# Attention units of a fused transformer layer issued as a fixed software pipeline

## The chip, the cores and the metric

The program runs on one core of one Trainium2 chip. Its time is the device time of one execution in microseconds (us). It is measured in whole executions; one more execution is recorded by the hardware profiler, and all rows below are of that one. TensorE (PE in the profile) does the matmuls and the transposes, VectorE (DVE) and GpSimd (POOL) elementwise work, ScalarE (ACT) activations and copies, and SyncE (SP) issues the DMAs. Matmuls write to PSUM, eight banks of 512 fp32 columns on 128 partitions.

## The reference

One layer of a hybrid backbone on 640 tokens: 512 latent tokens (group 0) and 128 prompt tokens (group 1). An adaLN map gives shift, scale and gate of each group; the normalised input goes through one input projection to four mixers; their outputs are projected, gated, summed and projected again; a squared-ReLU MLP follows.

```python
sh1, sc1, g1, sh2, sc2, g2 = jnp.split(mod, 6, axis=-1)          # adaLN
h = _rmsnorm(x, P['norm_mix_pre']) * (1 + sc1) + sh1
u = _split_cols(h @ P['w_in'])
o_a, st_a = _hgrn_mixer(u, P, lb_f, lb_b, ctx)                    # gated recurrence, 4 heads
o_b, st_b = _swa_mixer(u, P, pos, ctx)                            # window attention, 8 heads of 64
o_c, st_c = _mla_mixer(u, P, pos, ctx)                            # latent attention, 8 heads of 64 + 32
o_d, st_d = _gqa_mixer(u, P, pos, ctx)                            # grouped attention, 8 heads of 64
y = _merge((o_a, o_b, o_c, o_d), u['gates'], P)                   # sum of sigmoid(gate) * (o @ w_branch), @ w_out
x = x + g1 * _rmsnorm(y, P['norm_mix_post'])
...
y = jnp.square(jax.nn.relu(h @ P['w_mlp_in'])) @ P['w_mlp_out']
x = x + g2 * _rmsnorm(y, P['norm_mlp_post'])
```

Each attention is softmax(q k) v. Prompt tokens read prompt tokens only (128 keys). Latent tokens read 128 cached keys and the 512 latent keys (640 keys); in the window attention the cached ones and those up to 128 tokens away (384 or 512 keys), with a sink logit for each head.

## The kernel before

Activations are stored transposed (features on partitions) as pairs of a high and a low part, and each dense product is three matmuls: high times high, high times low, low times high. `t_steps` (line 357) makes a 128 x 640 block of a projection in two halves of 320 tokens; `tok_block` (line 375) makes a 128-token block in token order. Each weight tile of 512 KB is loaded by SP's queue (`wload`), its high part copied on GpSimd (line 139) and its low part made on VectorE (line 142).

PSUM is in pools: four banks for scores as two tiles of two banks (`sc_tile`, `sc_bank`), two banks for transposes and value products (`tp_tile`, `pv_tile`, one tag), two for projections (`mm_tile`, `mp_tile`, one tag).

The order of the instructions on each engine comes from a planner (it takes what its own costs say is ready, by priority in program order), except inside `in_order(...)`, which chains the named engines' instructions in the order in which the program writes them. Before the change this holds for the start and, for TensorE alone, for the first mixer (HGRN), where `beside(share)` takes so much dense work from a generator at each place. Stages by span time:

- 104 to 300: HGRN, two pairs of heads, seven levels each, with projections and `gate_steps(0)` beside them. A level is a block of matmuls, VectorE's product, two products on GpSimd (line 598), and VectorE again.
- 300 to 326: keys and first queries of the window attention, `merge(0)`. 326 to 478: its units, with the second pair's queries (`queries(1)`) and the gates (`gates(1)`) to be put between them by the planner.
- 478 to 526: keys and first queries of the grouped attention and `merge(1)`. 526 to 684: its units, second queries and `gates(3)`.
- 684 to 797: projections of the latent attention, `merge(3)`, `gates(2)`. 797 to 943: its four head pairs. Each has a prelude, written in front of its five units (lines 1142 to 1174): queries, rotary queries (five transposes), values of two pairs in every other one, keys. The projection banks are closed for this stage; one holds the adaLN accumulators, one is the prelude's `pj_tile`.
- To 1000: `gate_rows` and `merge(2)`; then the output projection, and from 1037 the MLP.

A `unit` (line 800) is one block of 128 queries for two heads: scores; per head a maximum, exponential with sum, reciprocal, and a weighing of P on GpSimd (`weigh`, line 809); transposes of P, four to a bank (line 856), copied out by ScalarE and VectorE in turn (lines 858, 860); value products into a bank of the same tag; `o_evac`. With 640 keys each head has its own two-bank score tile, filled in two pieces of 320. Each stage has 20 units, four of them on prompt tokens (one key tile). The score matmuls of the grouped kinds are two per piece and head (`qk_mm`), those of the latent one three (line 1182).

`q_split` (line 772) writes the high and the low part of a query block from PSUM. `side_steps(n)` runs `n` of the pending adaLN steps: each loads a weight tile of 512 KB and does four matmuls (line 211); in the latent attention three after every unit.

Of the kernel before, what the change touches and what calls it, by code (L numbers as in the profile page):

```python
# [20 lines left out]
T = TS + TP  # L21
# [43 lines left out]
def trunk(ctx, tc, I, O):  # L65
# [26 lines left out]
    pss = ctx.enter_context(tc.tile_pool(name="pss", bufs=2, space=PSUM))  # L92
# [3 lines left out]
    psm = [None, None]  # L96

    def open_mm():
        psm[1] = ExitStack()
        psm[0] = psm[1].enter_context(tc.tile_pool(name="psm", bufs=2, space=PSUM))  # L100

# [6 lines left out]
    def sc_tile():  # L108
        return pss.tile([128, 2, 512], F32, tag="sc", name="sc")
# [247 lines left out]
    def t_steps(w, m0, X, evac, halves=((0, HALF), (HALF, HALF)), bank=mm_tile):  # L357

        nk = len(w)
        for t0, tn in halves:  # L360
            ps = bank()
            for k in range(nk):
                wh, wl = w[k][0][:, m0:m0 + 128], w[k][1][:, m0:m0 + 128]
                a, b = X[k][0][:, t0:t0 + tn], X[k][1][:, t0:t0 + tn]
                PE.matmul(out=ps[:, 0:tn], lhsT=wh, rhs=a, start=(k == 0), stop=False)  # L365
                PE.matmul(out=ps[:, 0:tn], lhsT=wh, rhs=b, start=False, stop=False)  # L366
                PE.matmul(out=ps[:, 0:tn], lhsT=wl, rhs=a, start=False, stop=(k == nk - 1))  # L367
            evac(ps[:, 0:tn], t0, tn)
            yield 1.0
# [126 lines left out]
    V.tensor_scalar(out=nsink, in0=sink_b, scalar1=-1.0, scalar2=None, op0=ALU.mult)  # L496

# [190 lines left out]
    def gate_steps(n, sig):  # L688

        for kk in range(8):  # L690
# [5 lines left out]
            if kk % 4 == 3:  # L696
# [8 lines left out]
    with tc.tile_pool(name="hx", bufs=1) as hx:  # L705
# [25 lines left out]
        fill, due = dense(), 0.0  # L731

        def beside(share):

            nonlocal due
            due += share
            while due > 0:
                due -= next(fill, 100.0)

        with in_order(PE):  # L740
            for hp in range(2):
                lev = hgrn_levels(*qfk[hp], hx)
                while True:
                    try:
                        beside(next(lev))
# [3 lines left out]
                for share in hgrn_out(hp, *qfk[hp], A, QP, hx):  # L749
                    beside(share)  # L750
            for _ in fill:
                pass
# [47 lines left out]
    def unit(n, c, heads, qt, nk, score, pv_mm, sink=False, bands=None):  # L800
# [11 lines left out]
        if W > 512:  # L812

            for i in range(2):
                sv = sc_tile()[:, :, 0:W // 2]
                for a in range(2):
                    score(sv[:, a], i, a * (W // 2), W // 2)
                V.tensor_reduce(out=negm[:, i:i + 1], in_=sv, axis=AX.XY, op=ALU.max, negate=True)
                S.activation(out=Pt[:, i, 0:W].rearrange("p (a n) -> p a n", a=2), in_=sv, func=AF.Exp,
                             bias=negm[:, i:i + 1], accum_out=den[:, i:i + 1])  # L820
                V.reciprocal(out=rden[:, i:i + 1], in_=den[:, i:i + 1])  # L821
                weigh(i)
        else:
            sv = sc_tile()[:, :, 0:W]
# [26 lines left out]
        for j, kt in enumerate(range(0, nk, 2)):  # L851
            kn = min(2, nk - kt)
            tp = tp_tile().rearrange("p (k i) t -> p k i t", i=2)
            for i in range(2):
                for kk in range(kn):
                    PE.transpose(out=tp[:, kk, i], in_=Pt[:, i, 128 * (kt + kk):128 * (kt + kk) + 128], identity=ident)  # L856
            if j % 2 == 0:
                S.activation(out=PT[:, kt:kt + kn], in_=tp[:, 0:kn], func=AF.Copy)
            else:
                V.tensor_copy(out=PT[:, kt:kt + kn], in_=tp[:, 0:kn])  # L860
        o = pv_tile()
        for kt in range(nk):
            for a in range(2):
                pv_mm(o[64 * a:64 * a + 64, 0:128], a, kt, PT[:, kt, a], kt == 0, kt == nk - 1)
        o_evac(n, c, 128 * qt, o[:, 0:128])

    def gqa_like(n, qn, kn, ck, cv, ok, ov_, norm):
# [38 lines left out]
        def queries(j2):  # L906
            QQ = big(F32R, 2, 2, T, name="Q")
            Q = [QQ[:, a] for a in range(2)]
# [3 lines left out]
            for tt in range(NT):  # L912
                x = prepare(tt, ps, 4, norm and norm[0], None)
                if tt + 1 < NT:
                    ps = tok_block(wq, 256, hT, tt + 1, bank())

# [3 lines left out]
                q_split(tp[:, 0:2], [x[:, :, 128 * tt:128 * tt + 128] for x in Q], 0.125)  # L920
            return Q
        return queries, K, Vt
# [67 lines left out]
    def run_gqa(n, queries, Q0, K, Vt, tiles, sink, bands):  # L990
        for j2 in range(2):
            Q = queries(j2) if j2 else Q0
            for qt, i in [(qt, i) for qt in range(5) for i in range(2)]:
                ks, j = tiles(qt), 2 * j2 + i

                def score(out, a, k0, kn):
                    Qa = Q[a][:, i, 128 * qt:128 * qt + 128]
                    done = 0
                    while done < kn:
                        first = ks[(k0 + done) // 128] * 128 + (k0 + done) % 128  # L1000
                        step = 128 - (k0 + done) % 128
                        while done + step < kn and ks[(k0 + done + step) // 128] * 128 == first + step:
                            step += 128
                        step = min(step, kn - done)
                        qk_mm(out[:, done:done + step], Qa, K_part(K, first, step), a)
                        done += step

                def pv_mm(out, a, kt, PTa, start, stop):
                    PE.matmul(out=out, lhsT=Vt[:, ks[kt], 64 * a:64 * a + 64], rhs=PTa, start=start, stop=stop)  # L1009
# [333 lines left out]
```

## Time and profile before

| | |
|---|---|
| median of three executions | 1501.23 us (1500.88 to 1502.49) |
| profiled execution | 1502.2 us, span 1500.4 us, mean granted TensorE clock 0.991 |
| busy share of the span | PE 95%, DVE 53%, ACT 32%, POOL 29% |
| DMA | 121.17 MB, mean 81 GB/s |

The span runs from the first recorded instruction to the last. A busy share is that of the whole span, so it says nothing of a single stage; for that, the stretches below give each engine's busy time between two times of the span. In the chain of waits each step is what released the one after it. In a timeline, the bracket behind an instruction is the idle time of its engine just before it and what ended that.

### The profile page before, as it was taken

The numbers are of one execution on the slowest core, as the hardware profiler recorded it, in microseconds if no ns is written. First come the engines' busy times: TensorE is split into PE (matmuls) and PEld (weight loads), VectorE is DVE, ScalarE is ACT, GpSimd is POOL, SyncE is SP. The second block draws the span as 40 slices with busy tenths as digits, with TensorE's granted clock in tenths as the row PEclk, the third lists the DMA queues.
The fourth block names the chain that finished last, engine by engine and source line by source line (L and its number), as shares of the span: only waits on it lengthen the run. The fifth ranks groups of instructions, "written<-read, shape, count | busy, mean of one in ns | idle before, by whom it ended". The sixth has DMA issues, their size and how long they took to land.

```text
span 1500.4 us, 26709 instructions
## 1 busy us (share of the span) xinstructions
PE 1430.5 (95%) x10969; PEld 1302.2 (87%) x10969; DVE 796.1 (53%) x1447; ACT 481.4 (32%) x1161; POOL 432.2 (29%) x456
## 2 busy tenths in 40 slices
PE   6999999899999999999998998998999999999996
PEld 5898998899898998999996677988898998898995
DVE  4347657476643788433725566746243444444446
ACT  4334333333443235442124565225220110110112
POOL 2015325243321545222213334124111111112114
PEclk9999999999999999999999999999999999999998
DMA  9421212121112131112224601221343223222221
GB/s 328 128 85 58 70 49 64 50 68 50 45 43 59 34 84 37 33 42 74 80 68 143 224 15 43 99 85 56 112 129 101 80 71 98 71 70 71 75 66 70
DMA packets 138225, 121.17 MB, mean 81 GB/s; under 512 B 22296, under 2 KB 119412, under 8 KB 138104
## 3 DMA queue, kind: packets, MB, share of 16 engines
q1 hardware_dynamic: 138104, 119.47, 26.4%
q8 instruction: 86, 1.41, 0.4%
q14 instruction: 35, 0.29, 0.1%
HBM read 115.96 MB, written 3.49 MB: 80 GB/s over the span
## 4 chain that ended last, share of the span: by engine, by line
PE 70%; issue 13%; DVE 8%; POOL 5%; ACT 2%; DMA 1%; POOLq 0%; DVEq 0%; SPq 0%; ACTq 0%
PE mm L365 12%; PE mm L366 11%; PE mm L367 11%; PE mm L381 4%; PE mm L382 4%; PE mm L383 4%; PE tp L856 3%; POOL wh L139 3%; PE pv L1009 3%; PE sc L383 3%; PE sc L381 2%; PE sc L382 2%; PE sc L949 2%; PE sc L950 2%; DVE wl L142 1%
## 5 line engine op out<-in xcount | busy, mean ns | idle before, releaser
L139 POOL TENSOR_SCALAR wh<-wr 128x1024 fp32r<-128x1024 f32 (+3 forms) x136 | 156.7, 1154 | 536.4 <-PE mm L366 290.4
L142 DVE TENSOR_TENSOR wl<-wr,wh 128x1024 fp32r<-128x1024 f32 (+3 forms) x160 | 198.9, 1247 | 160.0 <-POOL wh L139 120.8
L365 PE MATMUL mm<-hTh,wh 128*128 128x320 f32 x704 | 220.5, 313 | 2.0 <-DVE qA L520 0.9
L367 PE MATMUL mm<-hTh,wl 128*128 128x320 f32 x704 | 219.2, 311 | 0.0
L366 PE MATMUL mm<-hTl,wh 128*128 128x320 f32 x704 | 218.2, 310 | 0.0
L366 PE MATMUL mm<-h2Tl,wh 128*128 128x320 f32 x512 | 159.4, 311 | 1.1 <-DVE h2Tl L142 1.1
L365 PE MATMUL mm<-h2Th,wh 128*128 128x320 f32 x512 | 159.5, 312 | 0.0
L367 PE MATMUL mm<-h2Th,wl 128*128 128x320 f32 x512 | 159.2, 311 | 0.0
L809 POOL TENSOR_SCALAR P<-P,rden 128x640 f32<-128x640 f32 (+3 forms) x120 | 84.5, 713 | 184.0 <-DVE rden L821 80.7
L365 PEld LDWEIGHTS mm<-hTh,wh 128*128 128x128 f32 x704 | 132.2, 188 | 3.9 <-DVE qA L520 1.0
L367 PEld LDWEIGHTS mm<-hTh,wl 128*128 128x128 f32 x704 | 132.2, 188 | 0.9 <-issue 0.7
L366 PEld LDWEIGHTS mm<-hTl,wh 128*128 128x128 f32 x704 | 132.2, 188 | 0.5 <-issue 0.3
L382 PE MATMUL mm<-wl,hidh 128*128 128x512 f32 x320 | 124.8, 390 | 0.6 <-DVE wl L142 0.6
L381 PE MATMUL mm<-wh,hidh 128*128 128x512 f32 x320 | 125.3, 392 | 0.0
L383 PE MATMUL mm<-wh,hidl 128*128 128x512 f32 x320 | 124.6, 389 | 0.0
L1292 ACT ACTIVATE relu<-mm 128x320 f32<-128x320 f32 x64 | 28.0, 438 | 281.1 <-PE mm L367 281.1
L366 PEld LDWEIGHTS mm<-h2Tl,wh 128*128 128x128 f32 x512 | 97.1, 190 | 1.7 <-DVE h2Tl L142 1.5
L365 PEld LDWEIGHTS mm<-h2Th,wh 128*128 128x128 f32 x512 | 96.9, 189 | 0.7 <-issue 0.4
L367 PEld LDWEIGHTS mm<-h2Th,wl 128*128 128x128 f32 x512 | 97.0, 189 | 0.0
L1293 DVE TENSOR_TENSOR relu<-relu 128x320 f32<-128x320 f32 x64 | 40.4, 632 | 100.8 <-ACT relu L1292 100.8
L1305 DVE TENSOR_TENSOR y<-mm,y 128x512 f32<-128x512 f32 x70 | 48.2, 689 | 81.9 <-PE mm L383 81.9
L381 PE MATMUL sc<-wh,hTh 128*128 128x256 f32 (+2 forms) x224 | 72.0, 322 | 5.5 <-DVE tx L935 2.4
(355 smaller groups left out, 3238.4 us busy)
## 6 DMA issues: line engine op xcount, KB each, us to landing
wr<-in_w_in SPq DMA_DIRECT2D x56, 512.0 KB, 3.7
wada<-in_w_ada SPq DMA_DIRECT2D x48, 512.0 KB, 4.5
wr<-in_w_mlp_in SPq DMA_DIRECT2D x32, 512.0 KB, 4.0
wr<-in_w_mlp_out SPq DMA_DIRECT2D x32, 512.0 KB, 3.6
wr<-in_w_in SPq DMA_DIRECT2D x64, 64.0 KB, 2.1
wr<-in_w_branch SPq DMA_DIRECT2D x8, 512.0 KB, 4.1
wr<-in_w_branch SPq DMA_DIRECT2D x16, 256.0 KB, 4.1
wr<-in_w_out SPq DMA_DIRECT2D x8, 512.0 KB, 3.6
```

The lines of the kernel that those rows point to most:

```text
L139: G.tensor_scalar(out=out, in0=src, scalar1=1.0, scalar2=1.0, op0=ALU.mult, op1=ALU.mult)
L142: V.tensor_tensor(out=out, in0=src, in1=f(hi), op=ALU.subtract)
L365: PE.matmul(out=ps[:, 0:tn], lhsT=wh, rhs=a, start=(k == 0), stop=False)
L366: PE.matmul(out=ps[:, 0:tn], lhsT=wh, rhs=b, start=False, stop=False)
L367: PE.matmul(out=ps[:, 0:tn], lhsT=wl, rhs=a, start=False, stop=(k == nk - 1))
L381: PE.matmul(out=ps[:, 0:n], lhsT=a, rhs=w[k][0], start=(start and k == 0), stop=False)
L382: PE.matmul(out=ps[:, 0:n], lhsT=a, rhs=w[k][1], start=False, stop=False)
L383: PE.matmul(out=ps[:, 0:n], lhsT=b, rhs=w[k][0], start=False, stop=(stop and k == nk - 1))
L809: G.tensor_scalar(out=Pt[:, i, 0:W], in0=Pt[:, i, 0:W], scalar1=rden[:, i:i + 1], scalar2=1.0, op0=ALU.mult, op1=ALU.mult)
L856: PE.transpose(out=tp[:, kk, i], in_=Pt[:, i, 128 * (kt + kk):128 * (kt + kk) + 128], identity=ident)
L1009: PE.matmul(out=out, lhsT=Vt[:, ks[kt], 64 * a:64 * a + 64], rhs=PTa, start=start, stop=stop)
L1305: V.tensor_tensor(out=ys, in0=ps, in1=ys, op=ALU.add)
```

## The change

Every attention unit is split into three functions: its scores with the softmax, `turn(part)` for the transposes (part 0 the first two banks, part 1 the third) and `products`. `run_units` issues them in rounds, with TensorE's order fixed: scores of a new unit, transposes of the unit before it, value products of the one before that, and after each part of the round a place for dense work. The dense work now comes in quarters of a half block: `t_steps` yields after every second weight block. In the window and the grouped attention `Fill.give(0.34)` at each place takes the second pair's queries and the gates in turn; units of prompt tokens (qt 4) stand third and seventh among the ten of a pair; the gates' sigmoids come after the last unit. In the latent attention the whole prelude of the first pair is made ahead of the units, in `sc_bank` and `mm_tile` in turn; those of the next pairs are the dense work (0.13 a place), two adaLN steps follow each value product, and the prompt unit stands third of five. All of PSUM but the transpose banks is laid out anew there: three banks in a row for the scores of both heads (cut at the banks into pieces of 512, 128, 384 and 256), one for adaLN, two for `pj`. The HGRN stage uses `Fill` too, with the same shares as before.

```diff
     def t_steps(w, m0, X, evac, halves=((0, HALF), (HALF, HALF)), bank=mm_tile):
...
                 PE.matmul(out=ps[:, 0:tn], lhsT=wl, rhs=a, start=False, stop=(k == nk - 1))
+                if k % 2 and k < nk - 1:
+                    yield tn / 1280
             evac(ps[:, 0:tn], t0, tn)
-            yield 1.0
+            yield (2 - nk % 2) * tn / 2560
...
+    class Fill:
...
+        def give(self, share):
+            self.due += share
+            while self.due > 0:
+                self.due -= next(self.steps, 1e9)
...
+        def softmax(i, sv, to, axis):
+            V.tensor_reduce(out=negm[:, i:i + 1], in_=sv, axis=axis, op=ALU.max, negate=True)
+            S.activation(out=to, in_=sv, func=AF.Exp, bias=negm[:, i:i + 1], accum_out=den[:, i:i + 1])
+            V.reciprocal(out=rden[:, i:i + 1], in_=den[:, i:i + 1])
+            weigh(i)
...
+        def wide_in():
+            k = 0
+            while k < 2 * W:
+                i, k0 = k // W, k % W
+                kn = min(W - k0, 512 - k % 512)
+                score(banks[:, k:k + kn], i, k0, kn)
+                k += kn
+            for i in range(2):
+                softmax(i, banks[:, W * i:W * i + W], Pt[:, i, 0:W], AX.X)
...
+        def turn(part):
+            for j, kt in list(enumerate(range(0, nk, 2)))[2 * part:2 * part + 2]:
...
+    def run_units(units, beside, after=lambda: None):
+        cur = old = None
+        units = iter(units)
+        with in_order(PE):
+            while True:
+                new = next(units, None)
+                if new is None and cur is None and old is None:
+                    break
+                if new:
+                    new[0]()
+                if cur:
+                    cur[1](0)
+                beside()
+                if cur:
+                    cur[1](1)
+                beside()
+                if old:
+                    old[2]()
+                    after()
+                beside()
+                old, cur = cur, new
...
+        def query_steps(j2, Q):
...
             for tt in range(NT):
                 x = prepare(tt, ps, 4, norm and norm[0], None)
                 if tt + 1 < NT:
                     ps = tok_block(wq, 256, hT, tt + 1, bank())
+                yield 0.8
...
                 q_split(tp[:, 0:2], [x[:, :, 128 * tt:128 * tt + 128] for x in Q], 0.125)
+                yield 0.1
...
+    def run_gqa(n, query_steps, Q0, K, Vt, tiles, sink, bands):
+        Q1, sig = [], [big(F32, 4, T, name="sig") for _ in range(2)]
+        second = query_steps(1, Q1)
+        def dense():
+            gate = gate_steps(n, sig, True)
+            for i, share in enumerate(second):
+                yield share
+                if i % 2 == 0:
+                    yield next(gate)
+            yield from gate
...
+                for qt, i in ((0, 0), (0, 1), (4, 0), (1, 0), (1, 1), (2, 0), (4, 1), (2, 1), (3, 0), (3, 1)):
...
+        fill = Fill(dense())
+        run_units(units(), lambda: fill.give(0.34))
+        fill.rest()
+        for g in sig:
+            S.activation(out=g, in_=g, func=AF.Sigmoid)
...
+        def heads(jj, got, bank):
...
+        banks = [sc_bank, mm_tile]
+        for _ in heads(0, got[0], lambda: banks.reverse() or banks[0]()):
+            pass
+        psm[1].close()
+        scores = psx.tile([128, 3, 512], F32, name="scores").rearrange("p a n -> p (a n)")
+        preludes = [None] + [heads(jj, got[jj], lambda: psx.tile([128, 512], F32, tag="pj", name="pj", bufs=2))
+                             for jj in range(1, 4)]
...
+                fill.rest()
+                fill.steps, fill.due = (preludes[jj + 1] if jj < 3 else iter(())), 0.0
+                for qt in (0, 1, 4, 2, 3):
+                    yield one(jj, qt, *got[jj])
...
-                side_steps(3)
+        run_units(units(), lambda: fill.give(0.13), lambda: side_steps(2))
```

## Rows read from the trace of the kernel before

**Rows 1.** Page: span; busy time and instructions by engine.
```profile
span 1500.4 us, 26709 instructions
...
PE 1430.5 (95%) x10969; PEld 1302.2 (87%) x10969; DVE 796.1 (53%) x1447; ACT 481.4 (32%) x1161; POOL 432.2 (29%) x456
```

**Rows 2.** Stretches: start:end, length, busy us of PE, PEld, DVE, ACT, POOL, granted clock, DMA.
```profile
104.00:300.00 196.00, 182.91 (x2420) 176.54 (x2419) 122.80 (x159) 74.68 (x154) 80.22 (x46) 1.00 0.22 61
326.00:478.00 152.00, 150.86 (x1153) 137.50 (x1152) 85.70 (x206) 61.52 (x174) 43.13 (x59) 1.00 0.21 53
478.00:526.00 48.00, 43.59 (x331) 42.09 (x331) 30.86 (x82) 14.39 (x34) 21.59 (x27) 0.96 0.17 41
526.00:684.00 158.00, 154.44 (x1285) 145.66 (x1283) 94.58 (x200) 67.42 (x172) 54.93 (x65) 1.00 0.19 49
...
797.00:943.00 146.00, 130.29 (x1122) 100.62 (x1121) 89.77 (x198) 83.29 (x227) 58.30 (x87) 0.98 0.32 105
```

**Rows 3.** Chain that ended last, latent attention: start, duration, work.
```profile
853.47 0.57 PE ada_ps L211 x8
...
886.73 1.96 PE mm L1203 x8
...
892.83 1.02 PE pv L1185 x16
...
925.75 1.02 PE pv L1185 x16
```

**Rows 4.** Timeline of one latent unit: start, duration, engine, line, instructions.
```profile
928.34 0.39 PE L949 MATMUL sc<-mK,mQ 128*128 128x320 f32 x1
...
929.15 0.31 PE L1182 MATMUL sc<-ckv,mQ 128*128 128x320 f32 x1
...
929.30 0.82 PE L856 MATMUL tp<-ident,P 128*128 128x128 f32 x6
...
929.50 0.82 DVE L818 TENSOR_REDUCE negm<-sc 128x1 f32<-128x640 f32 x1 [0.59 <-PE sc L1182]
929.71 0.60 ACT L858 ACTIVATE PT<-tp 128x512 f32<-128x512 f32 x1
...
930.31 0.67 DVE L860 COPY PT<-tp 128x512 f32<-128x512 f32 x1
...
931.14 1.31 PE L1185 MATMUL pv<-PT,qv 128*64 128x128 f32 x20
...
931.52 0.79 ACT L819 ACTIVATE P<-sc,negm 128x640 f32<-128x640 f32 x1
...
932.76 1.57 POOL L809 TENSOR_SCALAR P<-P,rden 128x640 f32<-128x640 f32 x2 [1.48 <-DVE rden L821]
...
932.79 0.31 PE L949 MATMUL sc<-Kp,mQ 128*128 128x128 f32 x1
...
932.94 0.27 PE L950 MATMUL sc<-Kp,mQ 128*128 128x128 f32 x1
```

**Rows 5.** Timeline: the first latent scores.
```profile
808.28 0.38 PE L949 MATMUL sc<-mK,mQ 128*128 128x320 f32 x1 [1.28 <-DVE Kp L142]
```

**Rows 6.** Groups by form, 797 to 945: count, busy, mean ns, idle before.
```profile
L365 PE MATMUL mm<-oh,wh 128*128 128x320 f32 x16 | 5.2, 333 | 1.6 <-DVE G L1206 1.4 <-DVE sig L980 0.2
```

**Rows 7.** Timeline around one window unit of 512 keys.
```profile
414.65 1.04 POOL L139 TENSOR_SCALAR wh<-wr 128x1024 fp32r<-128x1024 f32 x1
...
416.55 0.34 PE L950 MATMUL sc<-K,Q 128*128 128x384 f32 x1
...
421.27 1.36 POOL L809 TENSOR_SCALAR P<-P,rden 128x512 f32<-128x512 f32 x2 [5.57 <-DVE rden L847]
```

**Rows 8.** Timeline: one query tile of the second pair.
```profile
373.69 0.38 PE L919 MATMUL mp<-ident,txr 128*128 128x128 f32 x2
...
375.34 0.86 DVE L779 SCALAR_TENSOR_TENSOR Q<-mp,Q 64x256 fp32r<-64x256 f32 x2
```

**Rows 9.** Timeline of one level of the first mixer.
```profile
129.97 4.99 POOL L598 TENSOR_TENSOR hk<-hk,hf 128x640 f32<-128x640 f32 x2 [10.73 <-DVE hf L599]
```

More of the change, by code (lines that the diff above doesn't have):

```diff
@@ L749, in trunk @@
                 for share in hgrn_out(hp, *qfk[hp], A, QP, hx):
-                    beside(share)
-            for _ in fill:
-                pass
+                    fill.give(share)
+            fill.rest()
         wtile.act = False
@@ L798, in k_evac, with unit @@
             copy_r(Kt[rows[1 - a], a:4:2], f(Kt[rows[a], a:4:2]))
-    def unit(n, c, heads, qt, nk, score, pv_mm, sink=False, bands=None):
+    def unit(n, c, heads, qt, nk, score, pv_mm, sink=False, bands=None, banks=None):
         negm = sm.tile([128, 2], F32, tag="negm", name="negm")
@@ L986, in merge @@
                 t_block(wb, 128 * m, OT[n], ev)
[L990 to L1009, printed above, removed]
-                unit(n, j, (j, 4 + j), qt, len(ks), score, pv_mm, sink=sink, bands=bands(qt))
@@ L1012, in trunk, with units, one, score @@
-    queries, K, Vt = gqa_like(1, 'sq', 'sk', I['cache_swa_k'][0, 0], I['cache_swa_v'][0, 0], O['swa_k'], O['swa_v'], None)
+    def run_gqa(n, query_steps, Q0, K, Vt, tiles, sink, bands):
[8 more added lines that the diff above has]
+            yield from gate
+        def units():
+            for j2 in range(2):
+                for qt, i in ((0, 0), (0, 1), (4, 0), (1, 0), (1, 1), (2, 0), (4, 1), (2, 1), (3, 0), (3, 1)):
+                    if j2:
+                        for _ in second:
+                            pass
+                    yield one(Q1 if j2 else Q0, j2, qt, i)
+        def one(Q, j2, qt, i):
+            ks, j = tiles(qt), 2 * j2 + i
+            def score(out, a, k0, kn):
+                Qa = Q[a][:, i, 128 * qt:128 * qt + 128]
+                done = 0
+                while done < kn:
+                    first = ks[(k0 + done) // 128] * 128 + (k0 + done) % 128
+                    step = 128 - (k0 + done) % 128
+                    while done + step < kn and ks[(k0 + done + step) // 128] * 128 == first + step:
+                        step += 128
+                    step = min(step, kn - done)
+                    qk_mm(out[:, done:done + step], Qa, K_part(K, first, step), a)
+                    done += step
+            def pv_mm(out, a, kt, PTa, start, stop):
+                PE.matmul(out=out, lhsT=Vt[:, ks[kt], 64 * a:64 * a + 64], rhs=PTa, start=start, stop=stop)
+            return unit(n, j, (j, 4 + j), qt, len(ks), score, pv_mm, sink=sink, bands=bands(qt))
+        fill = Fill(dense())
+        run_units(units(), lambda: fill.give(0.34))
+        fill.rest()
+        for g in sig:
+            S.activation(out=g, in_=g, func=AF.Sigmoid)
+        return sig
@@ L1174, in mla @@
[L1174 to L1187 removed]
+                    yield 0.1
@@ new lines, in mla, with units, one, score @@
+        preludes = [None] + [heads(jj, got[jj], lambda: psx.tile([128, 512], F32, tag="pj", name="pj", bufs=2))
+                             for jj in range(1, 4)]
+        fill = Fill(iter(()))
+        def units():
+            for jj in range(4):
+                fill.rest()
+                fill.steps, fill.due = (preludes[jj + 1] if jj < 3 else iter(())), 0.0
+                for qt in (0, 1, 4, 2, 3):
+                    yield one(jj, qt, *got[jj])
+        def one(jj, qt, Qa, QR, K):
+            ks, Vt = full_tiles(qt), Vs[jj]
+            def score(out, a, k0, kn):
+                t = slice(128 * qt, 128 * qt + 128)
+                b = slice(ks[0] * 128 + k0, ks[0] * 128 + k0 + kn)
+                qk_mm(out, Qa[a][:, t], K_part(K, b.start, kn), a, last=False)
+                PE.matmul(out=out, lhsT=QR[a][:, t], rhs=KRo[:, b], start=False, stop=True)
+            def pv_mm(out, a, kt, PTa, start, stop):
+                PE.matmul(out=out, lhsT=Vt[:, ks[kt], 64 * a:64 * a + 64], rhs=PTa, start=start, stop=stop)
+            return unit(n, jj, (0, 1), qt, len(ks), score, pv_mm, banks=scores)
```

130 lines of the change are left out of this document (59 added, 71 removed).

## Prediction, made before the changed kernel ran

> **What bounds the kernel now.** First the page: TensorE is busy 95% of the span, no other engine over 53% [rows 1]. So the kernel gains where TensorE stands idle, and loses where it is made to wait. Next the stretches, one for each stage that the diff touches [rows 2]: the first mixer (104 to 300 us) is idle for 13.1 us, the window attention's units (326 to 478) for 1.1, the grouped attention's keys after them (478 to 526) for 4.4, the grouped units (526 to 684) for 3.6, and the latent attention with its four heads' preludes (797 to 943) for 15.7. The reader should see two kinds of attention stage there. The window and grouped units have gates and projections to put between them, and are nearly full. The latent ones are not: the chain of waits has one head's first value products at 892.83 and the next head's at 925.75, 33 us for five units [rows 3], where one unit's own work is about 4 (below). At the head change the next queries and keys are made while little else is left to run.
>
> The sum is made against the profiled execution's own time, 1502.2 us (span 1500.4 and 1.8 around it), 1.0 above the median 1501.2 of the three runs. A measurement of this kernel can tell about 0.2%, 3 us, from no change.
>
> **Latent attention, the part that should gain.** What one unit costs TensorE is read from a stretch without a hole: from 928.34 to 931.14, 2.8 us, twelve score matmuls and eight transposes are issued, then value products of 1.31; two transposes more (0.82 for six with their tail) make about 4.3 [rows 4]. After the change the 1280 score columns of both heads are cut at the banks as 512, 128, 384 and 256 instead of four times 320. Twelve matmuls stay twelve; 320 columns take 0.15 us (929.15 to 929.30), and a piece of 128 takes 0.11 to 0.15 (932.79, 932.94), not its 0.06 [rows 4]: 0.15 more. Both heads' scores in one go save about as much in change-overs: 4.3 again.
>
> Then the waits of the fixed order. Set t = 0 at the end of a unit's scores. The previous unit's first eight transposes take until 0.9 and fill both transpose banks. ScalarE's copy of the first bank (0.60) ends at about 1.25; only then do the last two transposes have a bank: 1.5. VectorE has the new unit's two maxima (0.82 each) before its own copy of the second bank (0.67): until 2.2. The value products use the same two banks, so they start at 2.25 and leave TensorE at 3.5; the next scores (1.9) end at 5.4. Exponentials (0.80 each, behind the copy) end near 2.9 and the two weighings on GpSimd (1.57 for both) near 4.1, before their transposes at 5.4 [rows 4]. So a full unit with nothing beside it takes 5.4 us, 1.2 of it waiting. Sixteen: 86.4. The four prompt units I put at 2.2 each (a fifth of the columns, short matmuls, and 0.6 for the next unit's weighing, which then comes too early): 8.8.
>
> The adaLN steps move from three after every unit to two after every value product. Each costs 0.57 [rows 3]; 24 and three short ones make 15.2, inside the order now. Their weights come over SP's queue at two 512 KB loads a round instead of three, so the order waits for them less, at most. The preludes of heads 2 to 4 are keys 6 matmuls of 384, queries 12 of 320, five transposes and, for one of the three, values of 18 matmuls of 256: at 0.15 us for 320 columns 1.1 + 1.8 + 0.6 three times, and 2.1, is 12.6. Two of their three places are exactly the two waits above, which can take 1.2 a round over some nine rounds; I take 8 as hidden, 4.6 left. Filling and draining the pipeline: 4, three quarters of a round. Sum 119.
>
> The first head's scores went on in earnest at 808.28 before, when the last keys were split [rows 5]. The first head's prelude now comes whole in front of them, on six banks instead of three; its evacuations on ScalarE and GpSimd set that start, and I leave it. Last value product then: 927.3. Two jobs that before lay in this stretch follow it: the gate rows (two groups of 1.96, of which 2 fit into the drain) and the 48 merge matmuls that were done by 945 (16 of each of three lines, 7.2 us) [rows 3, 6]. 927.3 + 1.9 + 7.2 = 936.4 against 945: **-9 us**. Bounds: if fill covers every wait, 11 us less (-20); if the exponentials always stand behind a prelude's copies and each round takes 6.2, 13 us more (+4).
>
> **Window attention.** A unit's softmax has to be done before its transposes, which now come exactly one round after its scores. For the widest unit the scores' last matmul starts at 416.55, and mask, maximum, two exponentials, sink and the weighing (421.27, 1.36 for both heads) are over at 422.63: 5.9 us after TensorE is free [rows 7]. A round has the previous unit's transposes, the value products of the one before, scores of about 1 and a dense share of 1.02 x 24 matmuls x 0.15 = 3.7: 5.9 to 6.4 us, the less where a prompt unit stands beside. So chain and round are about equal. I take 0.1 for 16 units, 1.5.
>
> The second pair's queries come into the order too. A gate half now keeps one of the two projection banks over four quarters, so query blocks and query transposes share the other: a block of the next tile waits until the transposes of this one are split. Before, that took from 373.69 to 376.20, 2.5 us [rows 8], and the next block had the other bank. By the shares (0.34 given, 0.8, 0.25 and 0.1 taken) this falls together at two of the five tiles: 5 us. The chain above runs on in that time, so half of it is bought back: 2.5. Against that, 1.1 of idle is all there is to win; I take 1 of it and let 1 of the 4.4 after it fill the two rounds that have no dense work: 1.5 + 2.5 - 2 = **+2**. Bounds -3 (all waits hidden) and +14 (rivals).
>
> **Grouped attention.** No mask or sink: the chain is that of rows 4, 4.1 us, against a round of over 6 (eight score matmuls 1.2, transposes 1.1, products 1.2, dense 3.7). No wait but the same two query hand-overs, 2.5 net, against 3.6 of idle of which I take 2.5: **0**, between -4 and +5. Moving the sigmoids behind the units takes ScalarE out of the units and puts it at each stage's end, beside key and projection work: nothing, at most 2 each.
>
> **First mixer.** Its dense work also comes in quarters. Groups of 24 and 48 matmuls become 36. But its idle time is set by GpSimd, whose two products take 5.0 us a level [rows 9], and by VectorE before and after them; a level takes that whatever the grain. **0**, between -3 and +2.
>
> **Sum.** -9 + 2 + 0 + 0 = -7: 1502.2 - 7 = **1495 us**. Own range 1491 to 1498.
>
> **Rivals.**
> - *The softmax sets the round in the window units (slower).* For: 5.9 against 5.9 to 6.4 is no margin, and a weight copy on GpSimd ahead of the weighing takes 1.04 [rows 7]. Against: such a copy comes every other round, and fits between two weighings. From a chain of 6.4 on it decides; at 7.0, 0.9 for each of 16 units, 14 us instead of 1.5: 1507.
> - *Nothing changes.* Rounds in the latent attention take 5.9, not 5.4, because ScalarE's queue has prelude copies in front of the exponentials: 16 x 0.5 = 8 back: 1503.
> - *The latent rounds are nearly full.* Preludes and adaLN work fall into the waits: 11 us more: 1484.
> - *The score banks bind.* One set of three banks now serves all units, and the middle bank holds columns of both heads, so the next scores need both exponentials to be over. By rows 4 that is at 2.9, and TensorE comes back at 3.5 or later: no price. Two exponentials behind 1 us of prelude copies make it 3.9: 0.5 x 16, 1503 again.
>
> A sentence of the Trainium skill speaks for this last one: *PSUM — Partial Sum Buffer*, "Summary: rules for kernel authors", says to read a result while TensorE writes only from a different bank. By that rule the shared middle bank serialises matmul and exponential, and the time would be that of this rival; the trace of before has two sets and cannot show one.
>
> **How the numbers follow.** Forecast 0.42 (0.38 faster, 0.04 same), nearly full rounds 0.14, nothing changes 0.15 (0.12 same, 0.03 slower), window chain 0.24, score banks 0.05 (0.02 same, 0.03 slower). Together: faster than 1498.2 in 0.52, within 3 us in 0.18, slower in 0.30. The range leaves out a tenth on each side: on the low side the nearly full case with a little more, 1482, on the high side the window chain, 1509.
>
> **What the profile after would show.** Right: between 797 and 943 the idle time falls below 10 us, no 33 us between heads, a value product every 5.4 to 6.3; TensorE idle in the window stage at about 3; the waits named are for the transpose banks' copies. Wrong: transposes of P waiting for GpSimd's weighing by more than 10 us in all in the window stage; scores waiting for the exponentials; query blocks waiting for the query split by more than 10 in both stages; or granted clock below full in a stretch where it was full [rows 2].

## The result and the profile after

The changed kernel takes 1562.47 us (1558.81 to 1564.1, four runs) against 1501.51: a ratio of 1.0402, 95% interval 1.0386 to 1.0418. That is 61 us slower, where 7 us faster was forecast, and far above the upper end of the range (1509). Its profiled execution took 1564.1 us.

The first two lines of its page, to be read against [rows 1]: span; busy time of each engine.

```profile
span 1562.3 us, 26719 instructions
...
PE 1450.7 (93%) x10969; PEld 1326.6 (85%) x10969; DVE 798.8 (51%) x1447; ACT 477.9 (31%) x1161; POOL 434.9 (28%) x456
```

TensorE has the same 10969 matmuls, and its busy time rose by 20.2 us all the same. The other 41.7 of the 61.9 us are idle time. So there are two losses: waiting, and matmuls that take longer. The stretches tell where. They are cut at the same matmuls in both traces: the end of the first mixer, the last window value product, the last block of rotary queries, the last merge matmul of the latent branch (the start falls within 1 us of it). First before, then after; columns as in [rows 2].

```profile
300.00:484.00 184.00, 182.38 (x1412) 168.37 (x1410) 103.90 (x244) 74.09 (x202) 55.89 (x73) 1.00 0.21 54
484.00:802.00 318.00, 309.10 (x2335) 298.05 (x2333) 175.78 (x389) 105.60 (x273) 105.15 (x127) 0.99 0.21 57
802.00:974.00 172.00, 156.87 (x1281) 125.79 (x1280) 109.14 (x235) 85.73 (x232) 60.37 (x89) 0.98 0.33 107
```

```profile
299.00:504.00 205.00, 187.47 (x1412) 175.53 (x1410) 107.04 (x245) 73.01 (x204) 59.30 (x73) 0.96 0.19 48
504.00:838.00 334.00, 316.96 (x2326) 305.27 (x2324) 173.72 (x386) 103.97 (x270) 105.83 (x127) 0.96 0.21 54
838.00:1036.00 198.00, 165.58 (x1285) 136.72 (x1285) 109.41 (x238) 84.93 (x234) 60.02 (x90) 0.91 0.28 93
```

All three stages lose: 21, 16 and 26 us. Length less busy time gives the idle part: it grew from 1.6 to 17.5, from 8.9 to 17.0 and from 15.1 to 32.4. The rest, 5.1, 7.9 and 8.7 us, is busy time, and it goes with a lower granted clock: 1.00, 0.99 and 0.98 became 0.96, 0.96 and 0.91. Everything behind the latent stage's merge takes as long as before, and the first mixer's 288.9 us (from the start to its last product) became 287.5.

What TensorE waited for, by the view of waits of the changed kernel; columns are total, times, longest. First window units (362 to 504), then grouped (545 to 732), then latent (862 to 1002):

```profile
PE tp L880 <- POOL P L817: 9.1, 6, 4.5
PE mm L383 <- DVE Q L786: 5.9, 3, 2.2
...
PE mm L383 <- DVE Q L786: 6.7, 3, 2.6
PE mm L365 <- DVE sig L1040: 3.4, 1, 3.4
...
PE scores L1009 <- ACT P L822: 14.4, 9, 4.4
```

Transposes of P wait for the weighing; a query block waits for the split of the tile before it; the merge of the window branch, early in the grouped stage, waits for VectorE; latent scores wait for the exponentials of the unit before. The latent stage also starts later: its first scores come 13 us after the last rotary block (837.9 to 851.1), before 4.5 (801.9 to 806.4).

The lower clock, by form: matmuls of 256 columns just behind the first of the query waits (363.4 to 366.8), and the same line some us earlier (352.8 to 358). Columns: busy, mean ns of one.

```profile
L383 PE MATMUL mm<-wh,hTh 128*128 128x256 f32 x6 | 2.5, 421 | 2.2 <-DVE Q L786 2.2
...
L383 PE MATMUL mm<-wh,hTh 128*128 128x256 f32 x15 | 4.2, 283 | 0.0
```

In the first stretch the granted clock was 0.5 (1.2 GHz), in the second 1.0 (2.4 GHz). Between them TensorE had stood idle for 2.2 us. The records of pipelined matmuls overlap, so the price of one is read from start to start: 0.21 us (363.51 to 363.72) instead of 0.12 (355.23 to 355.35). The same goes with the 4.5 us wait in the window stage and the 3.4 in the merge. The length of a wait alone does not decide: the third query wait, 1.8 us until 380.1, had a half clock behind it, the second, 1.9 us until 371.9, and a prelude's wait of 2.8 us until 907.1 had none. The longest stretch at 0.5, 13.7 us from 841.2, lies over the first latent prelude. The Trainium skill's *TensorE: Matmul & The Clock Gate*, section "HAM oscillation — how this bites in real kernels", describes this for waits on DMA: a wait sends the array back to half rate, and the next stretch starts cold. The trace agrees for waits on other engines, with a granted clock of 0.5 behind most of the longer waits and a mean of 0.91 in the latent stage.

### The profile page after: what moved, and what is told of

Read it like the earlier page. It is cut to its first block, busy times and chain, and to the rows that moved or that the text cites. A ratio compares the mean times of both kernels' runs of the same rounds, so it can differ in the third digit from the quotient of the medians.

```text
span 1562.3 us, 26719 instructions
## 1 busy us (share of the span) xinstructions
PE 1450.7 (93%) x10969; PEld 1326.6 (85%) x10969; DVE 798.8 (51%) x1447; ACT 477.9 (31%) x1161; POOL 434.9 (28%) x456
## 5 line engine op out<-in xcount | busy, mean ns | idle before, releaser
L365 PE MATMUL mm<-hTh,wh 128*128 128x320 f32 x704 | 228.2, 324 | 3.6 <-DVE qA L536 2.9
L817 POOL TENSOR_SCALAR P<-P,rden 128x640 f32<-128x640 f32 (+3 forms) x120 | 89.9, 756 | 191.1 <-DVE rden L823 93.1
L880 PE MATMUL tp<-ident,P 128*128 128x128 f32 x456 | 72.5, 287 | 14.7 <-POOL P L817 10.1
```

Source lines behind the costliest of these rows:

```text
L817: G.tensor_scalar(out=Pt[:, i, 0:W], in0=Pt[:, i, 0:W], scalar1=rden[:, i:i + 1], scalar2=1.0, op0=ALU.mult, op1=ALU.mult)
```

## The experiments

Theory A: TensorE's order is now fixed, so every late operand becomes idle time in all three stages, and the clock falls behind it. Rivals: the three shared score banks are the cause; the pieces or the pipeline are slow in themselves. The table has medians, ratios to the kernel before (95% interval) and the three stage lengths of the profiled execution (cut as above, so before: 195.1, 317.7, 171.3; the first now includes the first queries). The same latent code gave 190 to 197 us in different runs, so a few us of one stage length say little.

| run | us | ratio | window | grouped | latent |
|---|---|---|---|---|---|
| changed kernel | 1562.5 | 1.0402 (1.0386 to 1.0418) | 215.9 | 334.3 | 197.2 |
| latent as before | 1533.0 | 1.0210 (1.0191 to 1.0229) | 214.3 | 332.3 | 170.2 |
| free order | 1520.7 | 1.0123 (1.0108 to 1.0138) | 192.3 | 323.5 | 187.3 |
| free order, two score sets | 1508.8 | 1.0039 (1.0029 to 1.0049) | 192.3 | 323.5 | 176.5 |
| free order, latent as before | 1503.1 | 1.0012 (1.0003 to 1.0021) | 192.3 | 324.5 | 168.4 |
| the same, grouped as before too | 1500.5 | 0.9992 (0.9982 to 1.0002) | 192.3 | 320.5 | 174.4 |
| the same, merge in pieces | 1501.5 | 1.0001 (0.9989 to 1.0013) | 193.6 | 321.7 | 169.7 |
| maxima first | 1553.2 | 1.0335 (1.0317 to 1.0353) | 212.9 | 334.3 | 193.1 |
| gate between | 1559.5 | 1.0383 (1.0366 to 1.0401) | 210.3 | 339.8 | 194.0 |
| two score sets | 1559.4 | 1.0386 (1.0372 to 1.0401) | 212.9 | 331.3 | 197.9 |
| query blocks in quarters | 1551.6 | 1.0335 (1.0320 to 1.0349) | 213.1 | 330.3 | 191.4 |
| merge among the units | 1544.6 | 1.0264 (1.0236 to 1.0293) | 200.3 | 329.6 | 190.1 |
| TensorE kept busy | 1561.6 | 1.0389 (1.0363 to 1.0414) | 214.4 | 331.2 | 198.2 |

### Which part: latent as before, and free order

The latent code and its pools go back to those of before, window and grouped stages keep the fixed order.

> The latent attention is put back to the kernel before (its own head-by-head preludes, two score sets of two banks); window and grouped attention and the first mixer stay as in the changed kernel. Theory A (TensorE's fixed order turns late operands into idle time in all three attention stages, and the granted clock halves after such idle stretches): the latent stage's part of the loss goes, 7.5 us in front of its units, 15 in them and 2 behind, so about 1538 us. Rival B (the shared three score banks cause the loss, the other stages only move work about): 1500 to 1506. Rival C (the loss sits in the window and grouped stages alone, the latent stage is only later): 1560.

1533.0: 29.5 us go, 27 of them in the latent stage. Nearly half of the loss is there; the window and grouped stages keep 19 and 15. The shared banks alone (rival B) are out, and so is rival C.

```diff
-        with in_order(PE):
+        with ExitStack():
             while True:
```

> As the changed kernel, but the rounds of the units are not chained on TensorE: the planner may interleave them with anything that is ready; pieces, pools and shares stay. Theory A: most of the window and grouped loss goes (37 us), the latent waits for the score banks stay in part: 1510 to 1530. Rival B (pieces and banks, not the order): 1550 to 1563. If the order fixed by hand were better than the planner's, above 1563.

1520.7: 42 of the 61 us go with this one line, all pieces kept. The stretches, cut at the same matmuls:

```profile
299.00:480.00 181.00, 178.62 (x1411) 169.13 (x1409) 105.39 (x244) 72.35 (x202) 58.72 (x73) 1.00 0.21 55
480.00:804.00 324.00, 312.67 (x2330) 300.85 (x2328) 177.98 (x387) 107.86 (x273) 104.94 (x127) 0.98 0.21 56
804.00:992.00 188.00, 164.75 (x1284) 132.30 (x1283) 109.89 (x237) 85.41 (x234) 61.76 (x90) 0.95 0.29 99
```

In the window stage idle time is 2.4 us again and the clock 1.00, and the stage is 3 us shorter than before: pieces and pipeline are not slow there, the fixed order is. The grouped stage stays 6 us behind, the latent one 16.

### The latent stage: exponentials, banks, prelude

The timeline of one round of the changed kernel without prelude work shows the wait for the exponentials:

```profile
944.61 0.28 PE L1282 MATMUL scores<-ckv,mQ 128*128 128x256 f32 x1
...
944.93 0.82 DVE L821 TENSOR_REDUCE negm<-scores 128x1 f32<-128x640 f32 x1 [1.14 <-PE scores L1282]
...
945.85 0.79 ACT L822 ACTIVATE P<-scores,negm 128x640 f32<-128x640 f32 x1 [0.26 <-DVE negm L821]
...
946.77 0.16 DVE L823 RECIPROCAL rden<-den 128x1 f32<-128x1 f32 x1 [1.01 <-ACT P L822]
946.85 0.80 DVE L821 TENSOR_REDUCE negm<-scores 128x1 f32<-128x640 f32 x1
...
947.68 0.79 ACT L822 ACTIVATE P<-scores,negm 128x640 f32<-128x640 f32 x1 [0.78 <-DVE negm L821]
...
948.62 0.50 PE L1009 MATMUL scores<-mK,mQ 128*128 128x512 f32 x1 [1.27 <-ACT P L822]
```

The unit before this one is a prompt unit, with two transposes only. Between full units with no prelude or adaLN work left, as behind the scores of 967.65, the exponentials take as long, TensorE is back 3.0 us after the scores and waits 0.8. The first head's maximum starts after the last score of both heads. On VectorE the second maximum stands behind the first head's reciprocal, which waits for the first exponential. The second exponential is over at 948.57 (with the 0.19 us read of its sum), 3.7 us after the scores, and the next scores wait for it. Their first matmul writes only the first bank, which the second exponential does not read.

The longest of the nine waits, 4.4 of the 14.4 us, has one more piece in that queue. Columns as in the timeline above:

```profile
954.20 1.04 POOL L139 TENSOR_SCALAR wh<-wr 128x1024 fp32r<-128x1024 f32 x1 [4.53 <-DMA wr<-in_w_branch]
955.28 1.23 DVE L142 TENSOR_TENSOR wl<-wr,wh 128x1024 fp32r<-128x1024 f32 x1 [2.88 <-POOL wh L139]
...
956.49 0.80 DVE L821 TENSOR_REDUCE negm<-scores 128x1 f32<-128x640 f32 x1
...
958.27 0.80 PE L1009 MATMUL scores<-mK,mQ 128*128 128x512 f32 x1 [4.37 <-ACT P L822]
```

The planner had put the split of a merge weight in front of the reciprocal and the second maximum. VectorE stood idle for 2.9 us until GpSimd had copied that weight, and GpSimd had waited for its DMA.

```diff
...
             for i in range(2):
-                softmax(i, banks[:, W * i:W * i + W], Pt[:, i, 0:W], AX.X)
+                V.tensor_reduce(out=negm[:, i:i + 1], in_=sv[i], axis=AX.X, op=ALU.max, negate=True)
+            for i in range(2):
+                S.activation(out=Pt[:, i, 0:W], in_=sv[i], func=AF.Exp, bias=negm[:, i:i + 1],
+                             accum_out=den[:, i:i + 1])
+            V.reciprocal(out=rden, in_=den)
...
```

> As the changed kernel, but in the latent units both maxima are written before the exponentials and one reciprocal comes after both, so that VectorE's queue no longer holds the second maximum behind the first reciprocal. Theory A1 (that queue order makes the second exponential end 3.7 us after the scores, and the next scores wait for it): 1 us off each of 16 rounds that wait, less the clock: 1545 to 1553. Rival A2 (ScalarE's copies in front of the exponentials set it): unchanged, 1559 to 1564.

1553.2, 9 us less, at the edge of what A1 said. The waits for the exponentials fall from 14.4 to 4.3 us:

```profile
PE scores L1016 <- ACT P L845: 4.3, 4, 1.9
PE tp L887 <- ACT PT L889: 3.0, 10, 0.3
...
PE tp L887 <- POOL P L817: 2.7, 6, 1.2
PE pv L1292 <- ACT PT L889: 1.9, 4, 0.5
```

But the first exponential now starts behind both maxima, so such a round is only 0.3 us shorter (5.58 from scores to scores, 5.90 in the changed kernel), and part of the wait comes back at the copies and the weighing. The profiled execution shows 4 us of the gain in this stage. So the order of maxima and reciprocal is part of it, not 1 us a round; the 4.4 us wait is gone in this run, and how much of the gain is that weight's place in the queue is not shown.

```diff
-        scores = psx.tile([128, 3, 512], F32, name="scores").rearrange("p a n -> p (a n)")
+        psm[2] = ex.enter_context(tc.tile_pool(name="pss2", bufs=2, space=PSUM))
...
-        preludes = [None] + [heads(jj, got[jj], lambda: psx.tile([128, 512], F32, tag="pj", name="pj", bufs=2))
+        preludes = [None] + [heads(jj, got[jj], lambda: psx.tile([128, 512], F32, tag="pj", name="pj"))
...
-            return unit(n, jj, (0, 1), qt, len(ks), score, pv_mm, banks=scores)
+            return unit(n, jj, (0, 1), qt, len(ks), score, pv_mm)
```

> As the changed kernel, fixed order and pipeline kept, but the latent scores go to two sets of two banks, one for each head, in pieces of 320 as before; the preludes of heads 2 to 4 then have one bank instead of two. Theory A (the next scores wait for both exponentials because one set of three banks serves all units, 15.7 us of waits): these waits go, some come back at the one prelude bank: 1538 to 1550. Rival B2 (the round is as long without them, the time moves to P's transposes): 1556 to 1563.

1559.4: rival B2. The waits for the exponentials are gone, but others have their place, since the preludes have one bank:

```profile
PE pj L1235 <- DVE mQ L1241: 9.2, 3, 3.2
PE pj L365 <- DVE mK L142: 4.9, 2, 2.5
```

The same pools with the order left to the planner:

> All rounds left to the planner, latent scores in two sets of two banks with one prelude bank, preludes in pieces. Theory A: with the banks and the order of the kernel before back, only the pieces are new, and the latent stage is within 3 us of before (171.3 us with its merge, 187.3 in the free run with the shared banks): 1502 to 1508. Rival B3 (the pipeline's turn order and pieces cost by themselves): 1511 to 1521.

1508.8, a little above theory A's range: 12 us less than the free order with shared banks, 11 of them in the latent stage. So both layouts cost under the fixed order, each at its scarce bank, and the two sets cost little once the planner may put other work into their waits. The Trainium skill's *PSUM — Partial Sum Buffer*, "Summary: rules for kernel authors", asks, where a result is read while matmuls run, for a different bank, or at least a different quadrant. In these runs two sets were worth 12 us, but the wait above also held a bank that nobody read, so they do not show that the bank itself is what binds.

### Window and grouped stages: lumps and cover

Two gate quarters between a tile's transposes and the next query block:

```diff
-                if i % 2 == 0:
-                    yield next(gate)
+                if i % 2:
+                    yield next(gate)
+                    yield next(gate)
```

> As the changed kernel, but in the window and grouped stages two gate quarters (1.8 us of dense work) stand between a query tile's transposes and the next query block, instead of one in front of the transposes. Theory A3 (the block waits for the query split because both use the one free projection bank, six waits of 12.6 us in all, and each takes the clock down): waits fall below 4 us, and the half clock in these stretches with them: 1543 to 1552. Rival A4 (the time only moves to the wait of P's transposes for the weighing): 1557 to 1564.

1559.5: rival A4. The window stage's wait for the split is gone, but the wait for the weighing grew from 9.1 to 12.3 us (the view of waits, 355 to 504):

```profile
PE tp L880 <- POOL P L817: 12.3, 7, 4.4
```

In the grouped stage the transposes now wait 6.5 us for their own query rows.

Then the query blocks come in quarters too (`tok_steps` is `tok_block` with a yield of 0.2 after every second weight block), and one gate quarter stands also in front of the transposes:

```diff
-                    ps = tok_block(wq, 256, hT, tt + 1, bank())
-                yield 0.8
+                    ps = bank()
+                    yield from tok_steps(wq, 256, hT, tt + 1, ps)
+                yield 0.0
...
```

> As the run with the gate quarters between transposes and query blocks, but the query blocks too come in quarters, so that no place of a round gets 24 matmuls and the next none. Theory A5 (the waits for the weighing come in rounds that got no dense work because the block before was given whole): in the window stage the 12.3 us of waits for the weighing fall to about 4, half clock there goes: 1540 to 1550. Rival A6 (the softmax chain is longer than any round with a prompt unit in it): 1555 to 1562.

1551.6, between the two. The waits for the weighing by the same view, and the timeline of the longest, which shows its cause:

```profile
PE tp L890 <- POOL P L827: 10.8, 12, 5.1
```

```profile
436.89 1.28 ACT L1108 ACT_TABLE_LOAD   x1
...
438.19 2.34 ACT L1108 ACTIVATE sig<-sig 128x2560 f32<-128x2560 f32 x1
...
440.54 1.28 ACT L876 ACT_TABLE_LOAD   x1
441.83 0.20 ACT L876 ACTIVATE es<-es 128x2 f32<-128x2 f32 x1
...
443.41 1.03 PE L890 MATMUL tp<-ident,P 128*128 128x128 f32 x3 [5.09 <-POOL P L827]
```

The planner put half of the gates' sigmoid, with a table load on either side, in front of a unit's sink term: 4.9 us. Without it 5.7 us of the 12.3 are left, so the lumps were about half of the waits (A5), and something else is the other half.

The other half is cover. Between the first and the last window value product, before, TensorE had 91 us of dense matmuls (each counted at its full-speed slot, 0.147 us for 320 columns, and so on), among them half of the first mixer's merge (14 us); after, 64, because the merge is written ahead of the rounds and most query blocks fall before the first value product. So the merge becomes the first dense work of the rounds, at 0.475 a place instead of 0.34:

```diff
-    merge(0, False, sig0)
...
+            yield from ahead
             gate = gate_steps(n, sig, True)
...
-        run_units(units(), lambda: fill.give(0.34))
+        run_units(units(), lambda: fill.give(give))
```

> As the run with query blocks in quarters, and the first mixer's merge (192 matmuls, 28 us, done ahead of the window rounds in the changed kernel) becomes the first dense work of the window rounds, 0.475 a place instead of 0.34. Theory A7 (the planner of the kernel before had 91 us of dense work among its window units, the fixed rounds only 64; that cover hid the softmax): waits for the weighing in the window stage below 3 us, stage 195 to 200 us instead of 213, time 1533 to 1541. Rival A8 (the waits come from the order on VectorE's and ScalarE's queues, whatever the cover): 1546 to 1553.

The wait for the weighing falls to 0.7 us, the window stage from 213.1 to 200.3. The median is 1544.6, 7 us less (11 by the ratios); the profiled execution took 1538.4. Theory A7 holds for the wait, and for the stage at the edge of its range; the total is above its range.

```profile
PE tp L890 <- POOL P L827: 0.7, 3, 0.3
```

```profile
300.00:490.00 190.00, 181.54 (x1415) 170.30 (x1413) 105.99 (x245) 73.06 (x206) 57.59 (x73) 0.99 0.20 52
```

The chain is not constant either. This is the changed kernel in front of its 4.5 us wait:

```profile
386.24 0.39 PE L1010 MATMUL sc<-K,Q 128*128 128x512 f32 x1
...
387.31 1.39 DVE L142 TENSOR_TENSOR wl<-wr,wh 128x1024 fp32r<-128x1024 f32 x1
...
388.62 1.21 DVE L856 TENSOR_REDUCE negm<-sc 128x2 f32<-128x1024 f32 x1
...
390.44 0.86 DVE L786 SCALAR_TENSOR_TENSOR Q<-mp,Q 64x256 fp32r<-64x256 f32 x2
...
394.02 1.36 POOL L817 TENSOR_SCALAR P<-P,rden 128x512 f32<-128x512 f32 x2 [6.41 <-DVE es L865]
...
394.77 0.69 PE L880 MATMUL tp<-ident,P 128*128 128x128 f32 x2 [4.46 <-POOL P L817]
```

The unit's scores are over at 386.6 and its second weighing at 395.4: 8.8 us, with a weight split and a query split between its steps on VectorE. The chain alone does not decide, though: another unit's took 9.7 us (from 452.4) and no transposes waited for it, and with the merge among the units chains of up to 8.7 us leave no wait over 0.3.

### The clock

98 matmuls of no use, 14 behind the value products of each of the last seven latent rounds, into the unused half of the adaLN bank:

```diff
...
+            for _ in range(14 if len(turns) > 13 else 0):
+                PE.matmul(out=ada_ps[:, half], lhsT=kv3[:, 0, 0:128], rhs=kv3[:, 0, 128:384], start=True, stop=True)
```

> As the changed kernel, with 14 matmuls of 256 columns of no use behind the value products (and adaLN steps) of each of the last seven latent rounds, 98 in all, about 12 us of TensorE work, where TensorE otherwise waits for the exponentials. They write the unused half of the adaLN accumulators' bank; outputs are unchanged. Theory K (the granted clock falls because TensorE stood idle): between 940 us and the last value product the half-clock periods (13.6 us long in all in the changed kernel) mostly go, the waits shrink by what was filled, and the time is 1556 to 1564 in spite of the added work. Rival K2 (the clock falls for another reason): the periods stay and the time is 1566 to 1575.

1561.6, no longer than without them. From 940 to 1002, first the changed kernel, then this one:

```profile
940.00:1002.00 62.00, 48.54 (x392) 38.68 (x390) 26.85 (x59) 22.23 (x62) 15.88 (x23) 0.89 0.27 88
```

```profile
940.00:1002.00 62.00, 55.03 (x460) 46.33 (x460) 25.72 (x56) 19.94 (x53) 14.62 (x19) 0.97 0.30 102
```

The clock rises from 0.89 to 0.97. Not all of that is the filling: the useless matmuls start at 959.4, and the wait before, 4.4 us in the changed kernel, was 2.2 here. So the same in the rounds that are filled throughout, from the seventeenth unit's scores to the last value product, the changed kernel first:

```profile
967.60:1001.70 34.10, 28.21 (x214) 23.20 (x214) 13.03 (x28) 11.03 (x30) 6.31 (x9) 0.90 0.04 15
```

```profile
961.20:992.50 31.30, 28.81 (x261) 24.68 (x259) 10.41 (x24) 10.92 (x31) 6.35 (x9) 1.00 0.04 16
```

The clock is full where the waits are filled, and the rounds are 2.8 us shorter with the useless matmuls in them: theory K. The total does not gain from it: gate rows and merge matmuls that had stood in those waits come behind them now. About 12 us of added work (98 at 0.12 us) cost nothing.

### Versions against the kernel before

Three sums of edits shown above: the free order with the latent code of before; the same with the grouped units written unit by unit as before; and that with the merge and the query blocks of the window stage in pieces.

> Rounds of the window and grouped units left to the planner, latent attention as in the kernel before. Theory A: the two halves add up: 1520.7 less the 16 us by which the latent stage of the free run is longer than before: 1503 to 1507, the grouped stage 5 us behind the kernel before and the window stage 3 ahead. If the pipeline in quarters is itself slower, above 1510; if the planner uses it better than whole units, below 1500.

> First mixer and window units in quarters with the rounds left to the planner, grouped and latent attention as before. By the free run's window stage (192.3 us between its last first-mixer product and its last value product, against 195.1 before) and 1 us of the first mixer: 1496 to 1499. If that gain is only work moved to the next stage: 1500 to 1503.

> First mixer and window units in quarters, the first mixer's merge and the query blocks too, all left to the planner; grouped and latent attention as before. If the cover that hid the softmax under the fixed order (the merge among the rounds) also helps the planner, the window stage is at 189 to 192 us against 192.3 in the run without it and 195.1 before: 1495 to 1499. If the planner had that cover already (it put half of the merge among the units by itself): 1499 to 1502.

The halves add up: 1503.1 as theory A says. With the grouped stage planned as before too, 1500.5 misses the 1496 to 1499 that theory gave and lies where the second case, work only moved to the next stage, had put it. The window stage has 192.3 us in all four free runs with its merge ahead, against 195.1 before, but grouped and latent stage, with the code of before, are 3 us longer each in this trace (320.5 and 174.4; the execution took 1503.9), and the total can't be told from before. With the merge in pieces nothing more comes (1501.5): the planner had that cover already. No version beats the kernel before by what a measurement can tell.

## Why the prediction was wrong

The runs account for the loss in steps, by the ratios and in this order of taking back: 42 us for the fixed order, 13 for the shared score banks, 4 for what else is new in the latent stage (preludes, pieces, adaLN steps, order of units; no run takes these apart), 3 for the grouped stage. In another order the steps differ: two score sets under the fixed order were worth 3 us at most (the intervals overlap). By stage the forecast missed about 35 us in the latent attention (26 for -9), 19 in the window stage (21 for +2) and 16 in the grouped one (16 for 0). Of its four signs of being wrong three came: scores that wait for the exponentials, query waits of 12.6 us in both stages, and a granted clock below full in the window stage; the waits for the weighing there stayed at 9.1, just under the 10 it names. The prediction's steps, in turn:

- **Latent, "no price" for the score banks.** The step that failed most. It put the exponentials at 2.9 us after the scores and TensorE's return at 3.5. Measured, between full units with nothing beside them (scores of 967.65): exponentials 3.7, TensorE back at 3.0. So the wait that the sum left out came, 14.4 us in nine rounds, and the wait that it priced, 1.2 a round for the copies of the transposes, hardly did: 3.9 us in all from 862 to 1002. The sum took both maxima as done one behind the other and left out the reciprocal between them, which waits for the first exponential; nor did it have weight splits in VectorE's queue, which made the longest wait. The score-bank rival named the wait and priced it at 8 us with a chance of 0.05.
- **Latent, the first prelude.** Its evacuations "set that start, and I leave it": 8.7 us, 13.2 between last projection and first scores instead of 4.5. Run on its own in front of the units, with nothing beside it, it waits at its own evacuations, on VectorE above all, and from 841 to 855 it runs at half clock.
- **Window, the softmax.** Chain and round were put about equal, at 0.1 a unit. 9.1 us of waits came instead of 1.5. The rounds are not equal: a query block given whole leaves the next places without work, and the cover among the units fell by 27 us. Nor is the chain always the 5.9 us read from one unit: it was 8.8 behind the longest wait. So the rival (1507; its own terms add up to 1508) had the right wait and, in that round, its condition, a chain longer than 6.4 us; but the run with the merge among the units hides chains of up to 8.7, so it is the chain against the cover, not the chain alone.
- **Query hand-over.** Two of five tiles and half bought back were forecast, 2.5 us a stage; three of five waited, 5.9 and 6.7 us. Nothing was seen to be bought back.
- **Sigmoids, "at most 2 each".** The single wait of 3.4 us in the merge comes at that place, but the trace has something else in front of it: VectorE had no hole from 543.7 until the wait ended at 549.1, with two weight splits and query work before the merge's product. ScalarE's table load was over at 544.1. So it is VectorE's queue again; that the sigmoids cost anything is not shown.
- **The clock.** It stood among the signs of a wrong forecast and had no price in the sum. Busy time rose by 20 us with the same matmuls, a third of the loss.
- **Right:** the first mixer (0, measured -1.4 and within the spread of the runs).

## What to carry over

An order written by hand for one engine is only as good as the order on the engines that feed it: ask of every place in the round what stands in front of the operand on VectorE and ScalarE, and try the same pieces with the order left free before judging them. Count the dense work that lies among the units before and after; work written ahead of a pipeline is cover taken out of it. Price a wait on TensorE with the slower matmuls behind it.

## What was not expected of the hardware

Single waits of 1.8 to 4.5 us, in a kernel whose TensorE is busy 93% of the span, stood ahead of stretches at half clock, though others of up to 2.8 us had none behind them. Matmuls of 256 columns then take 421 ns instead of 283, and 0.21 us instead of 0.12 from one start to the next. Filling the latent stage's waits with 98 useless matmuls kept the granted clock at 1.00 instead of 0.90 in the rounds that were filled, at no cost in time.
